# Regrouping the small products of a chunked recurrence and tying its fill work to it, in a hybrid decoder layer

## The chip, the cores and the metric

The kernel runs on one core of one Trainium2 chip. The metric is the time of one execution on the device in microseconds (us), as a median over runs. The inputs are one sequence of 4096 tokens of width 1024, in f32, and the parameters of one layer.

## The reference

One decoder layer with two groups of heads side by side. A normalised input goes through one combined projection. Group A is a recurrence over the tokens (8 heads of 64), group B a dilated sliding-window attention (8 heads of 64). Each is multiplied by a gate from the same projection; both go through an output projection, the residual and a last norm. Cut to what matters:

```python
h = _rmsnorm(x, norm_gain)
p = h @ w_in                       # r, k, v, decay, rate | z_a, q, k, v, z_b
...
def step(S, inp):                  # group A, per head, one token
    sa = einsum('bhvk,bhk->bhv', S, -kk_t)
    S = S * w_t + sa[..., None] * b_t + v_t[..., None] * k_t
    y = einsum('bhvk,bhk->bhv', S, r_t)
    return S, y
...
y_a = group_norm(y) + bonus        # then * silu(z_a)
y_b = dilated_attention(q, k, v)   # (window, dilation) = (128,1), (512,4), (2048,16); then * silu(z_b)
x = rmsnorm(x + concat([y_a, y_b]) @ w_out)
```

## The kernel before, in words

The program is traced into a dependency scheduler, which orders each engine's instructions by their place in the source and by priorities. It has four stages.

The front (to about 650 us) projects the inputs of group A and stores them in DRAM.

The recurrence, `rwkv`, takes the 4096 tokens in 16 iterations of 256, each of 4 chunks c of 64 tokens and 4 pairs p of heads. All its pieces are put into a list of events by `at(t, ...)`, with a nominal time t in units of fill steps; the list is sorted by t and emitted in that order. Pieces of the chain (the inverse, the recurrence's steps, the group norm) are emitted with a raised priority (`HP`), so that the scheduler may place them earlier than the code around them. An iteration has, per pair, the preparation at the offsets of the table `PRE` (`keys`, `decay`, `keys2`, `norms`, `queries`, `gram`, `keysT`, `valuesT`), then `inverse`, which solves a triangular system for each chunk (small products `pq`, L1047 and L1053), then 16 steps s = (c, p) of the chain, then `finish`, the group norm with its transposes `py` (L1120).

`gram(i, st, p, h)` makes the scores of keys and queries within a chunk for one head h of the pair, four products of 64 x 128 rows and columns `pg` (L947), and masks them on VectorE into `G` (L948). The first head uses the upper 64 rows of the array, the second the lower.

A step of the chain, `stage`, has three parts that nominally come one step apart. Part 0 multiplies the state S with the keys and queries KR (L1072, 128 x 128), adds for each head the product GV of masked scores and values (L1074, 64 x 64) and copies the result to Z on ScalarE (L1077). Part 1 copies values to UV (L1081), multiplies Z by the inverse Xn for each head (L1083, 64 x 64) and copies the result to UV (L1085). Part 2 has BKT, keys by UV, as one product of 128 x 128 (L1088), Gout, scores by UV, for each head (L1090, 128 x 64), VectorE's update of S in two halves (L1093), and ScalarE's copy of the outputs into Y (L1095). The three results of a step share one accumulator bank, tag "zy", of which there are 3 (`PSB[2]`).

TensorE's other work in this stage is the fill, `self.fill()`, a generator with 576 steps: projections of the attention's queries, keys and gates in blocks of 24 products `pj` (L737) and of its values in blocks of 24 products `pv` (L718). They accumulate in two banks, tag "proj", and are evacuated by ScalarE and VectorE (for the values `vt`, L728 and L729, and a store `vsc`, L730). The event list takes `UT` = 34 fill steps per iteration; the 32 that are left ("late") follow the last iteration.

Then comes the attention. Its first event closes the fill's memory pools, loads constants (`at`, L1192) and the first head's keys and queries (`km`, `qm`, `kst`, `qhh`), and starts the last gates (weights `wzs`, L347, inputs `xZ`, L353, products `pz`, L357) and the first head's row maxima (`sm`, L1277). The main scores (`st`, L1330 and L1338) follow. The output stage ends the program.

Of the kernel before, what the change touches and what calls it, by code (L numbers as in the profile page):

```python
# [12 lines left out]
F32 = mybir.dt.float32  # L13
# [3 lines left out]
ALU = mybir.AluOpType  # L17
# [35 lines left out]
UVE = 1  # L53
# [6 lines left out]
PRE = (1, 1.5, 3.5, 4, 4.2, 7, 7.2, 9, 9.2)  # L60
# [5 lines left out]
VCE = 0  # L66
# [8 lines left out]
UT = 34  # L75
PSP = 5
# [112 lines left out]
class Layer:  # L189
# [597 lines left out]
    def rwkv(self, then=None):  # L787
# [149 lines left out]
        def gram(i, st, p, h):  # L937

            BK, KR = st["BK", p], st["KR", p]
            if h == 0:  # L940
                st["G", p] = sp.tile([128, 2, NCK, 128], F32, tag="G", name=f"G{i}_{p}", bufs=NG)
            Gt = st["G", p]
            mask = cst[:, C_MASK:C_MASK + 256].rearrange("p (r n) -> p r n", r=2)
            pg = pp.tile([128, NCK, 128], F32, tag="m", bufs=PSB[1], name=f"pg{i}_{p}_{h}")
            hs = slice(h * 64, h * 64 + 64)
            for c in range(NCK):
                P.matmul(pg[:, c, :], lhsT=BK[hs, c, :], rhs=KR[hs, c, :], start=True, stop=True)  # L947
            V.tensor_mul(Gt[:, h].rearrange("p (g r) n -> p g r n", r=2),  # L948
                         pg.rearrange("p (g r) n -> p g r n", r=2),
                         mask[:, None].to_broadcast([128, NCK // 2, 2, 128]))  # L950
            if h == 0:
                return
# [106 lines left out]
        def stage(i, st, s, part):  # L1059

            c, p = s // 4, s % 4
            par = c % 2
            hb, kc = (64, 64) if par == 0 else (0, 0)
            hk, rc = 64 - hb, 64 - kc
            bs, ks = slice(hb, hb + 64), slice(hk, hk + 64)
            KR, Gt, BKT, Vt, WC = (st[x, p] for x in ("KR", "G", "BKT", "V", "WC"))
            halves = [slice(0, 64), slice(64, 128)]
            if part == 0:
                if s == 0:
                    st["Y"] = ip.tile([128, NCK // 2, 512], F32, tag="Y", name=f"Y{i}", bufs=2)  # L1070
                st["bank", s] = bank = pp.tile([128, 3, 128], F32, tag="zy", name=f"zy{i}_{c}_{p}", bufs=PSB[2])
                P.matmul(bank[:, 0], lhsT=KR[:, c, :], rhs=Sbd[p], start=True, stop=True)  # L1072
                for h, hc in enumerate(halves):
                    P.matmul(bank[bs, 0, hc], lhsT=Gt[ks, h, c, kc:kc + 64], rhs=Vt[ks, c // 2, hc],  # L1074
                             start=False, stop=True, skip_group_check=True, tile_position=(hk, hb))
                st["Z", s] = Z = sp.tile([128, 128], F32, tag="Z", name=f"Z{i}_{c}_{p}", bufs=3)
                S.copy(Z[bs], bank[bs, 0])  # L1077
            elif part == 1:
                bank, Z = st["bank", s], st["Z", s]
                st["UV", s] = UV = sp.tile([128, 128], F32, tag="UV", name=f"UV{i}_{c}_{p}", bufs=UVB)  # L1080
                (S.copy, V.tensor_copy, G.tensor_copy)[VCE](UV[ks], Vt[ks, c // 2])  # L1081
                for h, hc in enumerate(halves):
                    P.matmul(bank[bs, 1, hc], lhsT=st["Xn"][bs, p * 4 + h * 2 + c // 2, :], rhs=Z[bs, hc],  # L1083
                             start=False, stop=True, skip_group_check=True, tile_position=(hb, hb))
                (S.copy if UVE else V.tensor_copy)(UV[bs], bank[bs, 1])  # L1085
            else:
                bank, UV = st["bank", s], st["UV", s]
                P.matmul(bank[:, 2], lhsT=BKT[:, c, :], rhs=UV, start=False, stop=True, skip_group_check=True)  # L1088
                for h, hc in enumerate(halves):
                    P.matmul(bank[ks, 0, hc], lhsT=Gt[:, h, c, rc:rc + 64], rhs=UV[:, hc],  # L1090
                             start=False, stop=True, skip_group_check=True, tile_position=(0, hk))
                for hc in halves:
                    V.scalar_tensor_tensor(Sbd[p][hc, hc], Sbd[p][hc, hc], WC[hc, c:c + 1], bank[hc, 2, hc],  # L1093
                                           op0=ALU.mult, op1=ALU.add)
                S.copy(st["Y"][ks, c // 2, p * 128:(p + 1) * 128], bank[ks, 0])  # L1095
# [36 lines left out]
        fill = self.fill()  # L1132
        for i in range(n):
            st = {}
            B = U * i
            for j in range(U):
                at(B + j, next, fill, None)
# [3 lines left out]
            for p in range(4):  # L1141
                b = B + PSP * p
                for o, fn, args in zip(PRE, (keys, decay, keys2, norms, queries, gram, gram, keysT, valuesT),
                                       ((),) * 5 + ((0,), (1,)) + ((),) * 2):
                    at(b + o * PSS, fn, i, st, p, *args)
# [4 lines left out]
            for s in range(16):  # L1150
                for part in range(3):
                    at(t0 + dt * (s + part) + 0.01 * (2 - part), stage, i, st, s, part, hp=HP[1])
# [522 lines left out]
```

## Time and profile before

| | before |
|---|---|
| time, median of 3 runs | 3496.95 us (3493.99 to 3497.66) |
| the profiled execution: time / span | 3487.44 / 3485.7 us |
| mean granted clock of TensorE | 0.948 |
| busy: PE / DVE / ACT / POOL | 3169.3 / 2205.0 / 1874.9 / 1314.9 us |
| products of the fill, pj / pv | 5376 of 277 ns / 768 of 385 ns |
| state L1072 / GV L1074 / Xn L1083 | 512 / 1024 / 1024 passes, 111.2 / 114.7 / 103.3 us busy |
| BKT L1088 / Gout L1090 / gram L947 | 512 / 1024 / 1024 passes, 113.4 / 118.2 / 130.6 us busy |

PE is TensorE's matmuls, PEld its weight loads, DVE is VectorE, ACT ScalarE, POOL GpSimd and SPq SyncE's DMA issues. A row of the time line has the start, the duration, the engine, the source line, the operation, output<-inputs, and how many of them follow each other; square brackets give idle time before it and what ended that. A row of a group has its count, busy time, mean ns of one, and the idle time before. Matmuls are pipelined: a pass shows 220 to 280 ns, while the next begins after about half of that or less, so that lengths are read from one start to the next. An f32 product counts as two passes.

### The profile page before, as it was taken

The page shows a single profiled execution, that of the slowest core. Times are in us where ns is not written, and L with a number is a line of the kernel's source. Part 1 is how long each engine was busy: PE and PEld are TensorE (multiplying, and loading weights), DVE is VectorE, ACT ScalarE, POOL GpSimd, SP SyncE. Part 2 cuts the span into 40 slices and gives each one's busy share as a digit, 9 for nine tenths or more (in the row PEclk, how much of TensorE's full clock was granted, in tenths as well). Part 3 has the DMA queues.
Part 4 walks back from the last instruction along what each step waited for, and adds up shares of the span by engine and source line. Part 5 has one row for each costly group of instructions (what it writes and reads, how often), then busy time and mean ns, then how long its engine had stood idle before and what let it go on. Part 6 is the DMA issues. An engine that isn't in the chain of part 4 may idle for free. (4 is left out here: it accounts for less than half of the span.)

```text
span 3485.7 us, 74535 instructions
## 1 busy us (share of the span) xinstructions
PE 3169.3 (91%) x27788; PEld 2461.5 (71%) x27788; DVE 2205.0 (63%) x5525; ACT 1874.9 (54%) x4174; POOL 1314.9 (38%) x1357
## 2 busy tenths in 40 slices
PE   5989988999999999999999999897988888978788
PEld 4878877878878887888766676675877777833333
DVE  7866767566666777766566677544655555246666
ACT  6465555345655555566555455432666666833233
POOL 4423233232343333333322222201555555755555
PEclk8999999999999999999999999897999999989999
DMA  6243667564455554454533333557755555376563
GB/s 192 92 137 138 198 177 223 194 165 132 123 151 146 153 135 126 126 138 131 157 110 93 99 110 96 123 152 167 132 96 107 111 106 106 100 216 189 185 186 115
DMA packets 644874, 490.59 MB, mean 141 GB/s; under 512 B 329456, under 2 KB 570864, under 8 KB 639472
## 3 DMA queue, kind: packets, MB, share of 16 engines
q1 hardware_dynamic: 644512, 485.83, 51.8%
q8 instruction: 219, 3.59, 0.4%
q14 instruction: 143, 1.17, 0.1%
HBM read 307.65 MB, written 177.77 MB: 139 GB/s over the span
## 5 line engine op out<-in xcount | busy, mean ns | idle before, releaser
L737 PE MATMUL pj<-xF,wf 128*128 128x256 f16 x5376 | 688.6, 277 | 13.4 <-ACT qhl L748 11.3
L737 PEld LDWEIGHTS <-wf 128*128 128x128 f16 x5376 | 502.8, 99 | 109.1 <-issue 14.9
L1350 POOL TENSOR_TENSOR hl<-pt,hl 128x1024 f16<-128x1024 f32 x192 | 367.9, 1926 | 288.6 <-ACT hl L1348 238.6
L562 PEld LDWEIGHTS <-wF 128*128 128x128 f16 x4032 | 395.3, 99 | 98.1 <-issue 42.3
L1590 PE MATMUL o<-wo,yc 128*128 128x512 f16 x1344 | 325.1, 405 | 76.6 <-DVE uC L1610 52.0
L1284 DVE CUSTOM_DVE_ANT_0 jk<-sm,at 128x256 bf16<-128x256 f32 (+1 forms) x768 | 259.1, 389 | 177.4 <-PE sm L1277 175.0
L1341 ACT ACTIVATE pt<-st,pb,esc 128x512 f32<-128x512 f32 (+1 forms) x344 | 257.4, 775 | 195.7 <-PE st L1338 159.4
L1590 PEld LDWEIGHTS <-yc 128*128 128x128 f16 x1344 | 138.0, 104 | 257.9 <-issue 103.7
L562 PE MATMUL ps<-xb,wF 128*128 128x256 f16 x2304 | 280.9, 276 | 23.1 <-DVE c L579 9.4
L1360 PE MATMUL po<-hl,vt 128*128 128x128 f16 (+1 forms) x3528 | 291.5, 234 | 9.9 <-POOL hl L1350 5.2
L1360 PEld LDWEIGHTS <-vt 128*128 128x128 f16 x3528 | 251.7, 101 | 26.9 <-issue 11.1
L1093 DVE SCALAR_TENSOR_TENSOR S<-S,WC,zy 64x64 f32<-64x64 f32 x512 | 142.8, 279 | 196.5 <-PE zy L1090 151.4
L562 PE MATMUL ps<-xa,wF 128*128 128x256 f16 x1728 | 217.8, 276 | 16.3 <-DVE u L577 13.7
L1277 PE MATMUL sm<-km,qm 66*128 66x256 f16 (+1 forms) x768 | 133.4, 279 | 83.5 <-DMA vt<-vsc 40.5
L718 PE MATMUL pv<-wf,xF 128*128 128x512 f16 x768 | 188.5, 385 | 0.0
L1338 PE MATMUL st<-q,k 66*128 66x256 f16 (+1 forms) x768 | 185.0, 271 | 0.0
L1338 PE MATMUL st<-qhh,kst 128*128 128x256 f16 (+1 forms) x768 | 184.5, 270 | 0.0
L1348 ACT CAST hl<-pt 128x1024 f16<-128x1024 f32 x192 | 180.9, 951 | 5.6 <-PE po L1360 3.2
L1277 PEld LDWEIGHTS <-qm 66*128 66x128 f16 x768 | 78.7, 123 | 94.9 <-DMA vt<-vsc 36.0
L1081 ACT COPY UV<-V 64x128 f32<-64x128 f32 x256 | 75.3, 295 | 127.9 <-PE zy L1090 125.3
L1330 PE MATMUL st<-at 128*128 128x512 bf16 (+1 forms) x352 | 136.6, 392 | 1.0 <-ACT pt L1341 0.9
L865 POOL TENSOR_TENSOR l_sq<-sq,h_sq 128x256 fp32r<-128x256 f32 x64 | 54.4, 850 | 219.3 <-ACT h_sq L864 212.3
(287 smaller groups left out, 6953.9 us busy)
## 6 DMA issues: line engine op xcount, KB each, us to landing
xF<-xsc SPq DMA_DIRECT2D x96, 512.0 KB
prs<-o SPq DMA_DIRECT2D x96, 256.0 KB
krv<-prs SPq DMA_DIRECT2D x64, 384.0 KB
wr<-in_w_in_dram SPq DMA_DIRECT2D x33, 512.0 KB
xr<-in_x_dram SPq DMA_DIRECT2D x32, 512.0 KB
xZ<-xsc SPq DMA_DIRECT2D x64, 256.0 KB
gC<-gsc SPq DMA_DIRECT2D x16, 1024.0 KB
xo<-in_x_dram SPq DMA_DIRECT2D x32, 512.0 KB
```

Source lines behind the costliest of these rows:

```text
L562: P.matmul(ps[:, 0:HT], lhsT=w[:, u, q % HK, :], rhs=x[:, v, q % HK, :], start=(start and q == 0), stop=(q == 3 * HK - 1), skip_group_chec ...
L718: P.matmul(ps, lhsT=x[v][:, k, s * 128:(s + 1) * 128], rhs=self.fw["v", 2 * u + k // 4][:, k % 4], start=(q == 0), stop=(q == 23))
L737: P.matmul(ps, lhsT=self.fw[b][:, u, k, :], rhs=x[v][:, k, :], start=(q == 0), stop=(q == 23))
L1093: V.scalar_tensor_tensor(Sbd[p][hc, hc], Sbd[p][hc, hc], WC[hc, c:c + 1], bank[hc, 2, hc], op0=ALU.mult, op1=ALU.add)
L1277: P.matmul(ps[:, n % 2, 256 - w:], lhsT=tok(qm[0:66], d, c, n * 128, 128), rhs=chunks(km[0:66], d, c, lo, w), start=True, stop=True)
L1284: V.tensor_tensor_reduce(jk[:, :w], ps[:, r % 2, 256 - w:], mask[:, i, 256 - w:256], 1.0, -3e38, op0=ALU.add, op1=ALU.max, accum_out=mx[:, ...
L1338: P.matmul(ps[:, at_:at_ + w], lhsT=tok(lh, d, c, n * 128, 128), rhs=chunks(rh, d, c, q0 * 128, w), start=False, stop=not st, skip_group_c ...
L1341: S.activation(pt[:, to:to + at_], ps[:, :at_], AF.Exp, scale=esc[:, p:p + 1], bias=pb[:, 0:1])
L1348: S.copy(hl[:, 0, :n], pt[:, :n])
L1350: (G if nsp[0] % HLG[0] < HLG[1] else V).tensor_sub(hl[:, 1, :n], pt[:, :n], hl[:, 0, :n])
L1360: P.matmul(out, lhsT=v[:, b * VW + v0:b * VW + v0 + 128], rhs=rhs, start=start and v0 + part == 0, stop=True, skip_group_check=True)
L1590: P.matmul(ps, lhsT=x[:, v, q % HK, :], rhs=w[:, u, q % HK, :], start=(start and q == 0), stop=(q == 3 * HK - 1), skip_group_check=True)
```

## The change

Three things are changed. `gram` emits the products of both heads in turn, into two accumulators that it holds at once, and has one place less in `PRE`. The chain's `stage` is split into `with_state`, `solve` and `new_state`, which are emitted slot by slot: state(s), then new_state(s - 2), then `solve` with Xn(s - 1) and GV(s), head by head in turn. In `new_state` BKT becomes two products of 128 x 64; the one of the other half comes first and VectorE updates that half of S, then both Gout products, then BKT of the own half with its update. The last copy of a step, into Y, is kept as `st["out", s]`. And a fill step is taken by `step(i, j)`: within `issue_after`, which makes the ScalarE instructions that it emits stand behind a named instruction, here the Y copy of some step of the iteration before (or of the last step of the one before that). Two options that had one value each are dropped.

```diff
-PRE = (1, 1.5, 3.5, 4, 4.2, 7, 7.2, 9, 9.2)
+PRE = (1, 1.5, 3.5, 4, 4.2, 7, 9, 9.2)
+LEAD = 6
...
-        def gram(i, st, p, h):
+        def gram(i, st, p):
...
-            pg = pp.tile([128, NCK, 128], F32, tag="m", bufs=PSB[1], name=f"pg{i}_{p}_{h}")
-            hs = slice(h * 64, h * 64 + 64)
+            pg = [pp.tile([128, NCK, 128], F32, tag="m", bufs=PSB[1], name=f"pg{i}_{p}_{h}") for h in range(2)]
             for c in range(NCK):
-                P.matmul(pg[:, c, :], lhsT=BK[hs, c, :], rhs=KR[hs, c, :], start=True, stop=True)
+                for h, hs in enumerate((slice(0, 64), slice(64, 128))):
+                    P.matmul(pg[h][:, c, :], lhsT=BK[hs, c, :], rhs=KR[hs, c, :], start=True, stop=True)
...
-                P.matmul(bank[:, 2], lhsT=BKT[:, c, :], rhs=UV, start=False, stop=True, skip_group_check=True)
-                for h, hc in enumerate(halves):
-                    P.matmul(bank[ks, 0, hc], lhsT=Gt[:, h, c, rc:rc + 64], rhs=UV[:, hc],
...
-                for hc in halves:
-                    V.scalar_tensor_tensor(Sbd[p][hc, hc], Sbd[p][hc, hc], WC[hc, c:c + 1], bank[hc, 2, hc],
...
-                S.copy(st["Y"][ks, c // 2, p * 128:(p + 1) * 128], bank[ks, 0])
+            for h in (1 - own, own):
+                hc = halves2[h]
+                if h == own:
+                    for u, uc in enumerate(halves2):
+                        P.matmul(bank[ks, 0, uc], lhsT=Gt[:, u, c, rc:rc + 64], rhs=UV[:, uc],
...
+                P.matmul(bank[hc, 2, hc], lhsT=BKT[:, c, hc], rhs=UV[:, hc], start=False, stop=True,
+                         skip_group_check=True, tile_position=(0, hc.start))
+                V.scalar_tensor_tensor(Sbd[p][hc, hc], Sbd[p][hc, hc], WC[hc, c:c + 1], bank[hc, 2, hc],
+                                       op0=ALU.mult, op1=ALU.add)
+            st["out", s] = S.copy(st["Y"][ks, c // 2, p * 128:(p + 1) * 128], bank[ks, 0])
...
+        def step(i, j):
+
+            s = int((j - LEAD - CHN[0]) / CHN[1]) - 2
+            if s >= 0 and i > 0:
+                after = sts[i - 1].get(("out", s))
+            else:
+                after = sts[i - 2].get(("out", 15)) if i > 1 and j > LEAD else None
+            if after is None:
+                next(fill, None)
+            else:
+                with tc.issue_after(after.ins):
+                    next(fill, None)
...
-                at(B + j, next, fill, None)
+                at(B + j, step, i, j)
...
-            for s in range(16):
-                for part in range(3):
-                    at(t0 + dt * (s + part) + 0.01 * (2 - part), stage, i, st, s, part, hp=HP[1])
+            for s in range(18):
+                if s < 16:
+                    at(t0 + dt * s, with_state, i, st, s, hp=HP[1])
+                if s > 1:
+                    at(t0 + dt * s + 0.01, new_state, i, st, s - 2, hp=HP[1])
+                if s < 17:
+                    at(t0 + dt * s + 0.02, solve, i, st, s, hp=HP[1])
...
-                at(U * n + j, next, fill, None)
+                at(U * n + j, step, n, j)
```

What this makes of the engines' orders is shown at three places. A row names the line, the instruction, its output and its inputs (`zy_1_2` is the accumulator of step c = 1, p = 2; G, UV, BKT its operands), its size, and in brackets the engines for which it waits. The first place is TensorE in the middle of the fill, in iteration 7; before, BKT and Gout of three steps stand between fill products and the gram:

```order
L737 MATMUL pj_16_21245<-xF_0_20689,wf_5_15842 128x256
L1088 MATMUL zy_1_2_20085<-UV_1_2_20110,BKT_2_18373 128x128 [waits Activation_49]
L1090 MATMUL zy_1_2_20085<-UV_1_2_20110,G_2_18318 64x64 x2
L1088 MATMUL zy_1_3_20115<-UV_1_3_20141,BKT_3_18626 128x128 [waits Activation_49]
L1090 MATMUL zy_1_3_20115<-UV_1_3_20141,G_3_18575 64x64 x2
```

After, at the same step of the same iteration:

```order
L944 MATMUL pg_3_1_20113<-KR_3_20009,BK_3_20008 128x128 x3
L736 LDWEIGHTS wf_2_15571
L736 MATMUL pj_23_20536<-xF_0_20392,wf_2_15571 128x256
L1104 MATMUL zy_1_2_20190<-UV_1_2_20230,G_2_18414 64x64 [waits DVE_49]
L1104 MATMUL zy_1_2_20190<-UV_1_2_20230,G_2_18414 64x64
L1106 MATMUL zy_1_2_20190<-UV_1_2_20230,BKT_2_18469 64x64
L1106 MATMUL zy_2_0_20253<-UV_2_0_20314,BKT_0_17971 64x64 [waits Activation_49]
L736 LDWEIGHTS wf_2_15571
L736 MATMUL pj_23_20536<-xF_0_20392,wf_2_15571 128x256
```

Gout now waits for VectorE, and the halves of BKT stand apart, the first of the next step alone ahead of a fill product. The second place is TensorE at the last product of the fill (`pv`, iteration 15). Before:

```order
L718 MATMUL pv_1_30150<-wf_1_23380,xF_1_29862 128x512
L977 MATMUL po_2_28858<-h_rb_2_28737,ones 128x256 [waits Activation_49]
L1088 MATMUL zy_1_0_29026<-UV_1_0_29085,BKT_0_27221 128x128 [waits Activation_49]
L1090 MATMUL zy_1_0_29026<-UV_1_0_29085,G_0_27164 64x64 x2
L1088 MATMUL zy_1_1_29090<-UV_1_1_29138,BKT_1_27410 128x128 [waits Activation_49]
L1090 MATMUL zy_1_1_29090<-UV_1_1_29138,G_1_27380 64x64 x2
```

After:

```order
L717 MATMUL pv_1_30400<-wf_1_23540,xF_1_30103 128x512
L1104 MATMUL zy_1_0_30147<-UV_1_0_30201,G_0_28590 64x64 [waits DVE_49]
L1104 MATMUL zy_1_0_30147<-UV_1_0_30201,G_0_28590 64x64
L1106 MATMUL zy_1_0_30147<-UV_1_0_30201,BKT_0_28643 64x64
L1104 MATMUL zy_1_1_30179<-UV_1_1_30237,G_1_28820 64x64 [waits DVE_49]
L1104 MATMUL zy_1_1_30179<-UV_1_1_30237,G_1_28820 64x64
L1106 MATMUL zy_1_1_30179<-UV_1_1_30237,BKT_1_28851 64x64
L1070 MATMUL zy_1_2_30228<-S_8280,KR_2_28909 128x128 [waits Activation_49]
```

The steps named there are of iteration 14 before (its preparation of iteration 15, `po_2`, is still to come) and of iteration 15 after. The third place is ScalarE at the copies of that last product (`vt`). Before:

```order
L1095 COPY Y_28801<-zy_0_3_28987 64x128 [waits DVE_49]
L728 ACTIVATE vt_1_30226<-pv_1_30150 128x4x64 [waits DMAHW2_49,PE_49]
L1081 COPY UV_1_3_29185<-V_3_27902 64x128 [waits PE_49,Activation_49]
L1081 COPY UV_2_0_29208<-V_0_27226 64x128 [waits PE_49,Activation_49]
L1095 COPY Y_28801<-zy_1_0_29026 64x128 [waits DVE_49]
```

After:

```order
L1110 COPY Y_30013<-zy_1_2_30228 64x128 [waits DVE_49]
L1110 COPY Y_30013<-zy_1_3_30259 64x128 [waits DVE_49]
L1080 COPY UV_2_3_30416<-V_3_29334 64x128 [waits PE_49,Activation_49]
L727 ACTIVATE vt_1_30479<-pv_1_30400 128x4x64 [waits DMAHW5_49]
L1110 COPY Y_30013<-zy_2_0_30295 64x128 [waits DVE_49]
L1092 COPY Z_2_1_30336<-zy_2_1_30320 64x128 [waits PE_49]
L1092 COPY Z_2_2_30366<-zy_2_2_30344 64x128 [waits PE_49]
L727 ACTIVATE vt_1_30479<-pv_1_30400 128x4x64 [waits DVE_49]
```

The copies of the last fill product moved behind Y and Z copies of the chain's last iteration.

More of the change, by code (lines that the diff above doesn't have):

```diff
@@ L52 @@
 MXL = 32
-UVE = 1
 PSB = (2, 2, 3, 1)
@@ L65 @@
 UVB = 3
-VCE = 0
 PRN = 1024
@@ L1057, in inverse, with at_chunk @@
             st["Xn"] = Xn
-        def stage(i, st, s, part):
+        def at_chunk(st, s):
             c, p = s // 4, s % 4
[L1062 to L1072, printed above, removed]
-                for h, hc in enumerate(halves):
[L1074 to L1091, printed above, removed]
-                for hc in halves:
-                    V.scalar_tensor_tensor(Sbd[p][hc, hc], Sbd[p][hc, hc], WC[hc, c:c + 1], bank[hc, 2, hc],
-                                           op0=ALU.mult, op1=ALU.add)
-                S.copy(st["Y"][ks, c // 2, p * 128:(p + 1) * 128], bank[ks, 0])
@@ new lines, in at_chunk, with with_state @@
+            hb, kc = (64, 64) if c % 2 == 0 else (0, 0)
+            return (c, p, slice(hb, hb + 64), slice(64 - hb, 128 - hb), kc) + tuple(
+                st[x, p] for x in ("KR", "G", "BKT", "V", "WC"))
+        halves2 = [slice(0, 64), slice(64, 128)]
+        def with_state(i, st, s):
+            c, p, bs, ks, kc, KR, Gt, BKT, Vt, WC = at_chunk(st, s)
+            if s == 0:
+                st["Y"] = ip.tile([128, NCK // 2, 512], F32, tag="Y", name=f"Y{i}", bufs=2)
+            st["bank", s] = bank = pp.tile([128, 3, 128], F32, tag="zy", name=f"zy{i}_{c}_{p}", bufs=PSB[2])
+            P.matmul(bank[:, 0], lhsT=KR[:, c, :], rhs=Sbd[p], start=True, stop=True)
@@ new lines, in solve @@
+        def solve(i, st, s):
+            for h, hc in enumerate(halves2):
+                if s > 0:
+                    c, p, bs, ks, kc, KR, Gt, BKT, Vt, WC = at_chunk(st, s - 1)
+                    if h == 0:
+                        st["UV", s - 1] = UV = sp.tile([128, 128], F32, tag="UV", name=f"UV{i}_{c}_{p}", bufs=UVB)
+                        S.copy(UV[ks], Vt[ks, c // 2])
+                    P.matmul(st["bank", s - 1][bs, 1, hc], lhsT=st["Xn"][bs, p * 4 + h * 2 + c // 2, :],
+                             rhs=st["Z", s - 1][bs, hc], start=False, stop=True, skip_group_check=True,
+                             tile_position=(bs.start, bs.start))
+                    if h == 1:
+                        S.copy(UV[bs], st["bank", s - 1][bs, 1])
+                if s < 16:
+                    c, p, bs, ks, kc, KR, Gt, BKT, Vt, WC = at_chunk(st, s)
+                    P.matmul(st["bank", s][bs, 0, hc], lhsT=Gt[ks, h, c, kc:kc + 64], rhs=Vt[ks, c // 2, hc],
+                             start=False, stop=True, skip_group_check=True, tile_position=(ks.start, bs.start))
+                    if h == 1:
+                        st["Z", s] = Z = sp.tile([128, 128], F32, tag="Z", name=f"Z{i}_{c}_{p}", bufs=3)
+                        S.copy(Z[bs], st["bank", s][bs, 0])
@@ new lines, in new_state @@
+        def new_state(i, st, s):
+            c, p, bs, ks, kc, KR, Gt, BKT, Vt, WC = at_chunk(st, s)
+            rc = 64 - kc
+            bank, UV = st["bank", s], st["UV", s]
+            own = ks.start // 64
+            for h in (1 - own, own):
[3 more added lines that the diff above has]
+                        P.matmul(bank[ks, 0, uc], lhsT=Gt[:, u, c, rc:rc + 64], rhs=UV[:, uc],
+                                 start=False, stop=True, skip_group_check=True, tile_position=(0, ks.start))
+                P.matmul(bank[hc, 2, hc], lhsT=BKT[:, c, hc], rhs=UV[:, hc], start=False, stop=True,
[3 more added lines that the diff above has]
+            st["out", s] = S.copy(st["Y"][ks, c // 2, p * 128:(p + 1) * 128], bank[ks, 0])
@@ L1142, in rwkv @@
                 b = B + PSP * p
-                for o, fn, args in zip(PRE, (keys, decay, keys2, norms, queries, gram, gram, keysT, valuesT),
-                                       ((),) * 5 + ((0,), (1,)) + ((),) * 2):
-                    at(b + o * PSS, fn, i, st, p, *args)
+                for o, fn in zip(PRE, (keys, decay, keys2, norms, queries, gram, keysT, valuesT)):
+                    at(b + o * PSS, fn, i, st, p)
             gen = inverse(i, st)
```

16 lines of the change are left out of this document (8 added, 8 removed).

## The prediction

> **What bounds the kernel now.** I read the span first, then the engines' busy time by stage, then the time line at both ends of the recurrence's last stretch. The page begins:
>
> ```profile
> span 3485.7 us, 74535 instructions
> ```
>
> The busy time by stage: start and end of the stretch, its us, then for each engine busy us and instructions (PE, PEld, DVE, ACT, POOL), the clock granted to TensorE, DMA share, GB/s.
>
> ```profile
> 650.00:1040.00 390.00, 375.84 (x3511) 313.89 (x3509) 246.70 (x522) 210.22 (x598) 128.22 (x145) 0.98 0.53 143
> 1040.00:1430.00 390.00, 383.29 (x3657) 316.50 (x3656) 276.17 (x582) 226.48 (x662) 131.29 (x143) 0.99 0.51 141
> 1430.00:1820.00 390.00, 381.85 (x3448) 299.61 (x3447) 264.38 (x582) 219.35 (x641) 125.29 (x156) 0.97 0.48 131
> 1820.00:2150.00 330.00, 327.63 (x2634) 226.94 (x2634) 217.96 (x498) 172.08 (x514) 84.51 (x145) 0.99 0.37 104
> 2150.00:2210.00 60.00, 60.00 (x529) 42.48 (x527) 38.75 (x68) 30.36 (x87) 15.86 (x27) 1.00 0.28 75
> 2210.00:2250.00 40.00, 32.66 (x229) 24.98 (x227) 22.44 (x78) 19.18 (x67) 5.27 (x10) 0.76 0.74 127
> 2250.00:2300.00 50.00, 40.68 (x408) 34.15 (x409) 30.14 (x74) 11.61 (x27) 2.90 (x1) 0.85 0.64 184
> 2300.00:2360.00 60.00, 60.00 (x549) 49.12 (x547) 20.52 (x85) 26.26 (x85) 2.90 (x4) 1.00 0.49 138
> 2360.00:2400.00 40.00, 34.68 (x291) 28.75 (x290) 24.51 (x119) 12.80 (x30) 6.38 (x11) 0.89 0.64 186
> ```
>
> From 650 to 2210 us, where the projections (the fill) and the recurrence share TensorE, it is busy 1528.6 of 1560 us: 31 idle. From 2210 to 2400 it is busy 168.0 of 190: 22 idle. The stage that the change touches is bound by TensorE's queue, and 53 us of it are idle. Its two ends, on TensorE:
>
> ```profile
> 2209.43 0.47 PE L977 MATMUL po<-h_rb,ones 128*128 128x256 f32 x1
> ...
> 2399.32 0.61 PE L1330 MATMUL st<-at 128*128 128x512 bf16 x1
> ```
>
> The first row follows the last fill pass, which so ends near 2209.4; the second is the first main score of the attention. I call the 190 us between them the tail. Behind the first main score both kernels have the same work, which I take as unchanged. The time is then the fill's end, the tail and a constant: the change gains only where it takes away work of TensorE, or idle time.
>
> **Part 1, TensorE's work.** Two products on different row halves of the array run at once in the trace: at 1849.16 those of two steps start together, and their eight passes are over by 1849.54, 0.38 us. The 16 gram passes of one head pair, one head behind the other, take 678.22 - 676.57 = 1.65 us, 0.10 each.
>
> ```profile
> 676.57 1.71 PE L947 MATMUL pg<-KR,BK 64*128 64x128 f32 x16
> 678.22 0.83 PE L737 MATMUL pj<-xF,wf 128*128 128x256 f16 x6
> ```
>
> ```profile
> 1849.16 0.27 PE L1083 MATMUL zy<-Z,Xn 64*64 64x64 f32 x1
> 1849.16 0.27 PE L1074 MATMUL zy<-V,G 64*64 64x64 f32 x1
> ...
> 1849.54 0.71 PE L947 MATMUL pg<-KR,BK 64*128 64x128 f32 x4
> ```
>
> The gram is now written with its heads in turn, but the scheduler leaves few pairs so: neighbouring gram products change halves 265 times instead of 47, and 17 of 64 pairs alternate throughout. 218 more changes at one pass of 0.10 are -22 us.
>
> Against that stand the stretches of small products between fill passes. Here are steps of the recurrence in the fill: the first BKT pair comes behind a fill pass, the second behind the column-tiled Gout.
>
> ```profile
> 1501.08 0.39 PE L1088 MATMUL zy<-UV,BKT 128*128 128x128 f32 x2
> 1501.40 0.45 PE L1090 MATMUL zy<-UV,G 128*64 128x64 f32 x4
> 1501.77 0.49 PE L1088 MATMUL zy<-UV,BKT 128*128 128x128 f32 x2
> 1502.19 0.45 PE L1090 MATMUL zy<-UV,G 128*64 128x64 f32 x4
> ```
>
> The first pair takes 1501.40 - 1501.08 = 0.32, the second 1502.19 - 1501.77 = 0.42: leaving a tiled shape costs 0.10. I estimate as much, and a little for a longer first pass, for entering it, 0.23 a stretch. The order has 1009 tiled stretches in the fill before and 1088 after: 79 x 0.23 = +18. [...]
>
> The 256 BKT products of two passes become 512 halves, four passes of half the columns a step. Four Gout passes take 0.37 (1501.77 - 1501.40), two BKT passes 0.32 to 0.42: -0.05 to +0.05 a step, I take +0.02, +5 in all. Sum of the work: -22 + 18 + 5, about 0; with the ends of the last term -15 to +10. The two options that are dropped had the values that the new code writes out: nothing.
>
> **Part 2, work that moves ahead of the last fill pass.** Before, the fill runs ahead of the recurrence: behind its last pass stand 26 steps' worth of products, the inverse of iteration 15 and its last preparation; after, 11 steps' worth and none of the rest. One whole step on TensorE, and the inverse's groups in the tail:
>
> ```profile
> 2222.97 0.44 PE L1083 MATMUL zy<-Z,Xn 64*64 64x64 f32 x4
> 2223.34 0.49 PE L1072 MATMUL zy<-S,KR 128*128 128x128 f32 x2
> ...
> 2224.93 0.66 PE L964 MATMUL pb<-cst,BK 128*128 128x128 f32 x4
> ```
>
> ```profile
> L1047 PE MATMUL pq<-Tn,G 32*32 32x32 f32 x64 | 3.1, 214 | 0.0
> L1053 PE MATMUL pq<-Xn,Tn 32*32 32x32 f32 x64 | 2.9, 193 | 0.0
> ```
>
> The five kinds of product of a step fill 2224.93 - 2222.97 = 1.96 us. 15 x 1.96 = 29.4, the inverse 3.1 + 2.9 = 6.0, and one pair's gram of 1.65 with the transposes and small products of its preparation, which I put at 6 in all: +42 on the fill's end, with 36 to 46. This isn't lost; it leaves the tail.
>
> **Part 3, waits in the fill.** A fill step's ScalarE instructions (its evacuations) now stand behind the Y copy of a step of the iteration before; its loads on SyncE are not tied. ScalarE's queue is in order, so Z and UV copies of the recurrence stand behind a waiting evacuation too, and the next fill block waits for one of two accumulators. In new_state, Gout now waits for VectorE's update of the first half of S, which reads the accumulator that it writes. That update:
>
> ```profile
> L1093 DVE SCALAR_TENSOR_TENSOR S<-S,WC,zy 64x64 f32<-64x64 f32 x512 | 142.8, 279 | 196.5 <-PE zy L1090 151.4
> ```
>
> 0.28 us of work, and I estimate as much again for the way there and back: for 0.6 us TensorE needs other work. Counting TensorE's own work between the instruction that a wait hangs on and the waiting one, 6 waits have under 1.5 us before, and 135 after, 88 of them under 1 us. Where nothing covers such a chain, at the end of the fill, it costs this:
>
> ```profile
> 2241.59 0.80 PE L1072 MATMUL zy<-S,KR 128*128 128x128 f32 x2 [0.50 <-ACT Y L1095]
> ...
> 2245.37 0.80 PE L1072 MATMUL zy<-S,KR 128*128 128x128 f32 x2 [1.03 <-ACT Y L1095]
> ```
>
> Fill passes cover part of it elsewhere; if each of the 88 lacks 0.2 of its 0.6 us, that is 18, and I take +20. The low end is +5, since all such waits hold only 31 us now; the high end 88 x 0.5 = 44, with late evacuations 50.
>
> **Part 4, the new tail.** On SyncE the last values store, the attention's first load and the gates' weights, and on TensorE the first gate product and the group of them:
>
> ```profile
> 2213.70 0.32 SPq L730 DMA_DIRECT2D vsc<-vt  x1
> ...
> 2215.78 0.34 SPq L1192 DMA_DIRECT2D at<-in_attc_dram  x1
> ...
> 2241.46 0.39 SPq L347 DMA_DIRECT2D wzs<-wz  x1
> ```
>
> ```profile
> 2254.95 3.51 PE L357 MATMUL pz<-xZ,wzs 128*128 128x256 f16 x16 [8.17 <-DMA xZ<-xsc]
> ```
>
> ```profile
> L357 PE MATMUL pz<-xZ,wzs 128*128 128x256 f16 x768 | 95.8, 278 | 13.2 <-DMA xZ<-xsc 11.8 <-ACT zhZ L363 1.4
> ```
>
> The last values store comes 4.3 us behind the fill. After, the copies that it waits for stand behind three Y and two Z copies of the last iteration's chain: 9, at worst 15. Then 2 to the first load; from there to the gates' weights it is 25.7 us now, with 35 transfers, among them those of iteration 15's inverse, which wait for data, and 22 transfers after: 15. From the weights to the first gate product 13.5. In all 39, with 34 to 46. All 768 gate products now follow the last recurrence product; before, 528 stand among its last steps. They are 95.8 busy; their 64 loads of 256 KB, 16.8 MB, take 91 us at the 184 GB/s of the stretch from 2250. With the maxima beside them 102 to 118, I take 108, then 10 for the maxima's last waits. 39 + 108 + 10 = 157 instead of 190: -33.
>
> **Sum.** 0 + 42 + 20 - 33 = +29 us: the work stays, the idle time goes from 53 to about 80. The profiled execution took 3487.44 (its span and 1.7 around it), 9.5 below the median of 3496.95; the difference goes on the median: 3526. A measurement of this kernel can tell about 0.2%, 7 us, from no change.
>
> **Rivals.** A, the tail empties more than the waits take: work -10, waits +5, and a tail of 130 (25 to the gates, 102 for them, 3 behind): 42 - 10 + 5 - 60 = -23, 3474. It decides where the tail falls below 190 - 42 less the waits. For it: the granted clock is only 0.76 from 2210 to 2250, so there is time to win. Against it: the gates alone are bound by their loads, and iteration 15 filled that time. Chance 0.16.
>
> B, the regrouped products run side by side: each of 256 steps saves one stretch of 0.37 (2223.34 - 2222.97), -95: 3526 - 95 = 3431. Against it: the order has GV and Xn of neighbouring steps in turn only some 20 times, since Xn waits for ScalarE's Z copy. Chance 0.03. [...]
>
> C, the chain decides: fill that itself waits for the recurrence no longer hides the 88 tight waits, and each costs 1 us, as at 2245.37: +88 instead of +20, 3594. Against it: blocks of 24 fill passes stand ready at most places. Chance 0.10.
>
> D, no difference (3490 to 3504): the fill stretch loses what the tail gains. Chance 0.13.
>
> **How the numbers follow.** The forecast, slower by 7 to 60, has the rest, 0.58. With C slower is 0.68; same 0.13; faster with A and B 0.19. The forecast's own range, its terms' distances added as squares (down 15, 15, 12; up 10, 30, 15), is 3502 to 3561. The range leaves out B, C and under half of A, 0.20: 3475 to 3560.
>
> **What would show it.** Right: the last fill pass near 2270 and the first main score near 2428; some 20 us more idle time of TensorE in the fill, released by S (VectorE) and by Y or Z (ScalarE); all gate products behind the last recurrence product. Wrong: a fill end before 2240 (parts 2 and 3), a tail above 180 or below 140 (part 4), unchanged idle time in the fill (part 3), or a first main score at 2392 or before (the sign).

## The result, and the profile after

The changed kernel takes 3604.13 us (median of 4 runs, 3601.43 to 3615.99) against 3497.3 before: a ratio of 1.030, with a 95% interval of 1.028 to 1.033. The forecast had the sign, slower, but a quarter of the size: 29 us where 107 came, outside its range. The profiled execution after has a span of 3604.0.

Here is the stage that changed, for each kernel in two stretches: from 650 us to the last fill pass, and from there to the first main score (columns as in the prediction). Before:

```profile
650.00:2209.40 1559.40, 1528.01 (x13767) 1198.93 (x13764) 1043.96 (x2250) 858.29 (x2499) 485.16 (x615) 0.98 0.47 129
2209.40:2399.30 189.90, 167.94 (x1470) 137.12 (x1468) 96.92 (x348) 70.03 (x208) 17.46 (x26) 0.89 0.62 158
```

After:

```profile
650.00:2363.00 1713.00, 1633.15 (x14781) 1248.50 (x14778) 1084.81 (x2359) 887.44 (x2596) 490.08 (x630) 0.94 0.44 119
2363.00:2512.00 149.00, 119.85 (x1064) 101.96 (x1062) 55.03 (x249) 41.44 (x115) 6.99 (x14) 0.89 0.69 186
```

Three things are to be read. The fill ends 153.6 us later and the tail is 40.9 shorter; the first main score is 112.7 later, and what follows it 5.6 longer (1086.3 to 1091.9). In the first stretch TensorE is idle 79.9 us where it was 31.4. And its granted clock, the third column from the right, is 0.94 where it was 0.98. In the clock's records of these two traces it is always 1 or one half in this stage; the half adds up to 54.6 us before and 211.6 after. Fill products that follow each other start 0.21 us apart at half clock and 0.11 at full (medians of the trace after), so I take half of the time that TensorE is busy at half clock as lost. It is busy for 51.5 of those 54.6 us and for 187.3 of those 211.6: 25.7 lost before, 93.6 after.

That gives a ledger for every run of this study, from 650 us to the first main score: the idle time of TensorE, the time at half clock, the loss (idle time, and half of the busy time at half clock), and the rest, which is the work at full clock. For before: 53.4 idle, 96.7 at half clock (18.0 of it idle, which is counted already), loss 92.7, work 1656.6. After: 109.0 idle, 243.0 at half clock (43.5 of it idle), loss 208.8, work 1653.2. The loss grew by 116.1, the work shrank by 3.4, and their sum is the 112.7. A second kernel with the same order of TensorE (the state product behind new_state, below) has 7.0 more loss and 8.3 less work than the changed kernel, so differences below 10 us in the ledger say nothing.

One place of the changed kernel, on VectorE and TensorE, shows waits and the half clock that follows them:

```profile
861.80 1.89 DVE L1023 TENSOR_TENSOR pm<-XL,XH 128x1024 f32<-128x1024 f32 x1
...
862.96 0.33 PE L1106 MATMUL zy<-UV,BKT 128*64 128x64 f32 x2
863.60 0.27 DVE L1108 SCALAR_TENSOR_TENSOR S<-S,WC,zy 64x64 f32<-64x64 f32 x1
...
863.93 0.45 PE L1104 MATMUL zy<-UV,G 128*64 128x64 f32 x4 [0.65 <-DVE S L1108]
...
865.25 0.39 PE L1104 MATMUL zy<-UV,G 128*64 128x64 f32 x3 [0.39 <-DVE S L1108]
...
866.54 0.80 PE L1070 MATMUL zy<-S,KR 128*128 128x128 f32 x2 [0.73 <-ACT Y L1110]
...
881.84 5.42 PE L736 MATMUL pj<-xF,wf 128*128 128x256 f16 x27
```

The first half of BKT is done by 863.29; VectorE's update of S could follow, but stands behind an operation of the inverse that starts at 861.80 and takes 1.89, and Gout waits for the update. Within 4 us TensorE waits 0.65, 0.39 and 0.73. The clock falls at 866.1, during the third wait; the state product of 866.54 takes 0.80 where the median at full clock is 0.49 in this stretch. The clock in the three stretches around it:

```profile
862.70:866.10 3.40, 2.08 (x23) 1.39 (x21) 3.37 (x6) 0.75 (x3) 0.00 (x0) 1.00 0.00 0
866.10:886.60 20.50, 20.06 (x143) 15.74 (x144) 10.96 (x25) 11.61 (x34) 5.25 (x10) 0.50 0.26 56
886.60:906.60 20.00, 20.00 (x237) 17.13 (x236) 9.26 (x21) 12.65 (x36) 9.02 (x6) 1.00 0.59 165
```

After 1.32 us idle of 3.40 the clock is at half for 20.5 us, in which TensorE is busy 20.06: by the half taken above 10 us are lost, behind waits of 1.8. From the fall to 881.84 TensorE has only f32 products of the recurrence and its preparation; there a block of 27 fill products begins, and 4.8 us later the clock is full. All 19 such periods of the first stretch after, and 10 of the 11 before, have at least 0.36 us of idle time in the 8 us ahead of them; of the stretches of 8 us at full clock, taken every 2 us, 90 of 674 after and 60 of 708 before have as much. The waits of TensorE by what they wait for, first one row from before, then after:

```profile
PE zy L1072 <- ACT Y L1095: 1.9, 2, 1.5
```

```profile
PE zy L1070 <- ACT Y L1110: 24.7, 22, 3.4
PE pg L944 <- DVE BK L917: 10.6, 3, 8.7
PE zy L1104 <- DVE S L1108: 9.2, 14, 2.2
```

The state product's wait for the Y copy, which frees its accumulator, was 1.9 us before; Gout's wait for S did not exist.

### The profile page after: what moved, and what is told of

It reads as the page before. It is cut to its first block, busy times and chain, and to the rows that moved or that the text cites. A ratio compares the mean times of both kernels' runs of the same rounds, so it can differ in the third digit from the quotient of the medians.

```text
span 3604.0 us, 75138 instructions
## 1 busy us (share of the span) xinstructions
PE 3217.6 (89%) x28300; PEld 2465.9 (68%) x28300; DVE 2194.6 (61%) x5525; ACT 1873.3 (52%) x4174; POOL 1316.8 (37%) x1357
## 5 line engine op out<-in xcount | busy, mean ns | idle before, releaser
L736 PE MATMUL pj<-xF,wf 128*128 128x256 f16 x5376 | 708.8, 280 | 5.0 <-ACT qhl L747 4.1
L561 PE MATMUL ps<-xb,wF 128*128 128x256 f16 x2304 | 285.2, 278 | 26.0 <-DVE c L578 10.2
L1108 DVE SCALAR_TENSOR_TENSOR S<-S,WC,zy 64x64 f32<-64x64 f32 x512 | 137.1, 279 | 196.6 <-PE zy L1106 187.3
L1311 PE MATMUL sm<-km,qm 66*128 66x256 f16 (+1 forms) x768 | 130.8, 277 | 79.9 <-DMA kst<-qk 18.2
L1070 PE MATMUL zy<-S,KR 128*128 128x128 f32 x512 | 123.1, 324 | 28.0 <-ACT Y L1110 25.7
L1106 PE MATMUL zy<-UV,BKT 128*64 128x64 f32 x1024 | 144.5, 239 | 1.7 <-ACT UV L1085 1.7
L911 POOL TENSOR_TENSOR BK<-kk,sg 128x256 f32<-128x256 f32 x64 | 61.1, 955 | 221.1 <-DVE sg L887 176.2
```

Of the source, the lines that this page charges most:

```text
L561: P.matmul(ps[:, 0:HT], lhsT=w[:, u, q % HK, :], rhs=x[:, v, q % HK, :], start=(start and q == 0), stop=(q == 3 * HK - 1), skip_group_chec ...
L736: P.matmul(ps, lhsT=self.fw[b][:, u, k, :], rhs=x[v][:, k, :], start=(q == 0), stop=(q == 23))
L1106: P.matmul(bank[hc, 2, hc], lhsT=BKT[:, c, hc], rhs=UV[:, hc], start=False, stop=True, skip_group_check=True, tile_position=(0, hc.start))
```

## The experiments

The theory behind the runs: new bare waits of the chain, in its new order (1) or for want of fill where it is tied (2), bring idle time and with it half clock. The first four runs do each part alone, and all but the tie. The ratio is that to the kernel before on the same chip.

**The gram in turn, alone.**

```diff
-        def gram(i, st, p, h):
+        def gram(i, st, p):
...
+                for h, hs in enumerate((slice(0, 64), slice(64, 128))):
+                    P.matmul(pg[h][:, c, :], lhsT=BK[hs, c, :], rhs=KR[hs, c, :], start=True, stop=True)
```

> The kernel before with the gram's two heads in turn and nothing else. Theory 1 (the chain's new order makes the waits) and theory 2 (the tied fill makes them) expect the same here: the gram is no cause of the loss, 3475 to 3500 against 3497 before, with idle time of TensorE in the fill stretch of 25 to 40 us (31 before). A rival, that two accumulators held at once by one gram starve the preparation (tag m has two), expects over 3520 and waits of the gram on VectorE.

Measured 3473.2 against 3498.3, ratio 0.994 (0.992 to 0.996): 25 us faster, a little more than expected of it. The ledger has 22.9 less work. The rival of starved preparation, which expected over 3520, is out by the time; idle time in the fill is 43.5, just above the range expected.

**The chain's new order, alone.**

```diff
-                for part in range(3):
-                    at(t0 + dt * (s + part) + 0.01 * (2 - part), stage, i, st, s, part, hp=HP[1])
+            for s in range(18):
+                if s < 16:
+                    at(t0 + dt * s, with_state, i, st, s, hp=HP[1])
...
```

> The kernel before with the chain's new order (with_state, solve, new_state) alone: fill untied, gram by head. Theory 1 expects most of the loss: 3550 to 3600, over 60 us idle in the fill stretch, waits of the state product on ScalarE's Y copy and of Gout on VectorE's S, and over 150 us at half clock (55 before). Theory 2 expects 3485 to 3515 and idle time near 31, since untied fill still covers the waits.

Measured 3535.4, ratio 1.012 (1.010 to 1.015). Neither theory had it. The first stretch and the tail of this run:

```profile
650.00:2117.30 1467.30, 1445.89 (x13375) 1119.40 (x13372) 949.26 (x2073) 788.36 (x2299) 428.38 (x562) 0.99 0.48 132
2117.30:2457.90 340.60, 297.30 (x2499) 237.47 (x2498) 186.77 (x558) 138.27 (x413) 58.52 (x73) 0.76 0.45 110
```

With the fill untied, the scheduler fills the chain's waits with more fill: the first stretch has only 21.4 us idle and ends 92 us earlier. But 51 steps of the recurrence are left behind the last fill pass, and there the waits are bare: clock 0.76, tail 341 us. The cost of the new order is real, and moves to where the fill is not.

**The tie, alone.**

```diff
-                at(B + j, next, fill, None)
+                at(B + j, step, i, j)
...
-                S.copy(st["Y"][ks, c // 2, p * 128:(p + 1) * 128], bank[ks, 0])
+                st["out", s] = S.copy(st["Y"][ks, c // 2, p * 128:(p + 1) * 128], bank[ks, 0])
```

> The kernel before with the fill tied to the Y copies alone: chain and gram as before. Theory 1 expects 3490 to 3520: the fill's end later by some 40, the tail shorter by as much, idle time in the fill below 45. Theory 2 expects 3560 to 3600, with over 60 us idle and over 150 us at half clock, waits of fill products on ScalarE's evacuations among them.

Measured 3569.8, ratio 1.020 (1.016 to 1.024), as theory 2 expects:

```profile
650.00:2337.00 1687.00, 1612.87 (x14228) 1262.25 (x14226) 1090.83 (x2349) 886.98 (x2588) 505.76 (x626) 0.96 0.45 120
2337.00:2486.80 149.80, 122.77 (x1060) 103.22 (x1058) 57.33 (x255) 44.19 (x123) 8.17 (x16) 0.89 0.67 187
```

With the chain as before, the tie brings 74.1 us idle in the first stretch and the late end. The loss of the ledger grows by 75.9, the work by 11.6, hardly more than the ledger can tell; the first main score comes 87.5 later.

**The gram and the chain, fill untied.** The changed kernel with one line back:

```diff
-                at(B + j, step, i, j)
+                at(B + j, next, fill, None)
```

> The changed kernel with its fill untied (gram and chain as changed). Theory 1 expects 3550 to 3590; theory 2 expects 3480 to 3505; if both are needed (the chain's bare waits hurt only where the fill is held back), 3490 to 3520 here and the same in the two runs with one of them alone.

Measured 3532.0, ratio 1.011 (1.008 to 1.013), between the theories. Against this run the tie costs 73 us more. So the loss has two causes of its own, and theory 1 or 2 alone is not enough.

The next runs take up the chain's order. **The state product behind new_state:**

```diff
-                    at(t0 + dt * s, with_state, i, st, s, hp=HP[1])
+                    at(t0 + dt * s + 0.015, with_state, i, st, s, hp=HP[1])
```

> The changed kernel, with the state product of step s emitted behind new_state(s - 2) and not ahead of it. Theory 1a: the state product waits bare because only one solve stands between the Y copy that frees its accumulator and itself; with BKT and Gout in between, the waits of the state product on ScalarE's Y copy fall from 24.7 us to under 8, idle time in the fill from 80 to 60, half clock from 212 to 140 to 170, and the time from 3604 to 3545 to 3575. Theory 2 (the tied fill alone makes the idle time) expects no change, 3590 to 3615.

Measured 3613.4, ratio 1.031 (1.028 to 1.033): no gain, and the waits for Y are 25.3 us as before. But the run tells nothing of theory 1a: TensorE's order is the changed kernel's, instruction by instruction; the scheduler seems to place these products by priority and readiness and not by their place in the list. It is a second measurement of the changed kernel and shows how far two such agree (3604 and 3613). Theory 1a stays untested.

**BKT whole, Gout and both updates behind it**, the slots as changed:

```diff
+            P.matmul(bank[:, 2], lhsT=BKT[:, c, :], rhs=UV, start=False, stop=True, skip_group_check=True)
             for u, uc in enumerate(halves2):
                 P.matmul(bank[ks, 0, uc], lhsT=Gt[:, u, c, rc:rc + 64], rhs=UV[:, uc],
...
-                P.matmul(bank[hc, 2, hc], lhsT=BKT[:, c, hc], rhs=UV[:, hc], start=False, stop=True,
```

> The changed kernel with BKT again as one product, then Gout, then both updates of S; slots, gram and tie as changed. Theory 1b (Gout's wait for VectorE's update of the first half, which delays the Y copy and with it the next state product): the 9.2 us of Gout's waits go, those of the state product halve, 3550 to 3580. Theory 2 expects 3590 to 3615.

Measured 3544.1, ratio 1.011 (1.008 to 1.013): 60 us faster than the changed kernel. Gout's waits are gone, those for Y fall to 13.4. Idle time as a whole hardly falls (77.3 in the first stretch), since other waits grow, but the time at half clock does, from 211.6 to 122.9. Theory 1b holds, with a time just below its range; what Gout's wait costs comes mostly through the clock, and not through idle time.

Then the tie. **Only its far end** (the last Y copy two iterations back) **and only its near one:**

```diff
-            if s >= 0 and i > 0:
-                after = sts[i - 1].get(("out", s))
-            else:
-                after = sts[i - 2].get(("out", 15)) if i > 1 and j > LEAD else None
+            if True:
+                after = sts[i - 2].get(("out", 15)) if i > 1 and j > LEAD else None
```

> The kernel before with the fill tied only to the last Y copy two iterations back (from the seventh fill step of an iteration on). If the near tie makes the cost: 3495 to 3515, idle time in the fill 30 to 45, half clock 50 to 80. If any tie that stops the fill from running ahead costs: 3545 to 3575, as in the run with both.

```diff
-                after = sts[i - 2].get(("out", 15)) if i > 1 and j > LEAD else None
+                after = None
```

> The kernel before with the fill tied only to the Y copies of the last iteration's steps 0 to 8 (the fill steps from the 23rd on, and the late ones). If the near tie makes the cost: 3545 to 3580, with over 60 us idle and over 120 us at half clock in the fill. If the far one does: 3495 to 3520.

Measured 3595.6, ratio 1.025 (1.023 to 1.028), and 3569.9, ratio 1.019 (1.016 to 1.021). Each by itself costs about as much as both together or more (91 and 65 us, against 72), in the first stretch 68.7 and 70.0 idle and 177.5 and 150.2 at half clock. It isn't how near the tie is.

**The tie on TensorE's Gout and not on ScalarE's Y copy:**

```diff
-                    P.matmul(bank[ks, 0, hc], lhsT=Gt[:, h, c, rc:rc + 64], rhs=UV[:, hc],
+                    st["out", s] = P.matmul(bank[ks, 0, hc], lhsT=Gt[:, h, c, rc:rc + 64], rhs=UV[:, hc],
...
```

> The kernel before with the same tie as in the run with the tie alone, but fill steps stand behind the step's last Gout product on TensorE instead of its Y copy on ScalarE: TensorE's fill products are held back, ScalarE's queue is free. If holding the fill back costs: 3550 to 3585, idle time in the fill over 60 us. If it was ScalarE's queue (evacuations behind copies that wait, and Z and UV behind those): 3495 to 3525, idle time below 45 and waits of fill products on ScalarE near the 13 us of before.

Measured 3579.9, ratio 1.021 (1.018 to 1.024), with 78.0 idle and 139.9 at half clock. ScalarE's queue behind a waiting evacuation, which part 3 named, is not needed for the cost; the fill held back costs by itself.

**BKT whole and the fill untied:** the edits of two runs above together.

> The changed kernel with BKT whole (Gout behind it, then both updates) and the fill untied; the gram in turn and the slots stay. If the halves of BKT make the chain's cost: 3465 to 3485, as the gram alone (3473). If the slots make it (state ahead of new_state, heads in turn): 3520 to 3540, as with the halves and no tie (3532).

Measured 3501.0, ratio 1.000 (0.998 to 1.002), between the two expected. The slots give back the gram's 25 us, and the halves with the wait cost some 33 more, up to the ratio of the run with halves and no tie. Against this run the tie, with BKT whole, costs only 39 us (ratio 1.011 against 1.000).

**Gout first, then both halves of BKT, then both updates**, all else as changed:

```diff
             for u, uc in enumerate(halves2):
                 P.matmul(bank[ks, 0, uc], lhsT=Gt[:, u, c, rc:rc + 64], rhs=UV[:, uc],
                          start=False, stop=True, skip_group_check=True, tile_position=(0, ks.start))
+            for hc in halves2:
+                P.matmul(bank[hc, 2, hc], lhsT=BKT[:, c, hc], rhs=UV[:, hc], start=False, stop=True,
+                         skip_group_check=True, tile_position=(0, hc.start))
```

> The changed kernel with Gout ahead of both halves of BKT and the two updates behind them: the halves stay, the round trip over VectorE between them and Gout goes. If the round trip costs: 3535 to 3555, as with BKT whole (3544). If the halves themselves do (twice the passes, more stretches of small products): 3590 to 3610. An even split would be 3565 to 3580.

Measured 3518.1, ratio 1.004 (1.002 to 1.006), faster than any price named. The halves are not the cost; here, with no wait between them and Gout, they are a gain (3518.1 against 3544.1 with BKT whole). On TensorE, a step in the fill:

```profile
1502.40 0.27 PE L1100 MATMUL zy<-UV,G 128*64 128x64 f32 x1
1502.41 0.27 PE L1103 MATMUL zy<-UV,BKT 128*64 128x64 f32 x1
...
1502.68 0.28 PE L1103 MATMUL zy<-UV,BKT 128*64 128x64 f32 x2
1502.89 0.50 PE L736 MATMUL pj<-xF,wf 128*128 128x256 f16 x3
```

Passes of Gout and of the BKT half in the other columns start 10 to 20 ns apart where they stand in turn and run side by side: the eight take 0.49 us (1502.40 to 1502.89). Before, two whole BKT passes and four of Gout take 0.69 (0.32 + 0.37 in the prediction's rows) to 0.79. The ledger has 80.8 less work than before. It also has more idle time, 133.1, presumably because less work covers the same waits.

So two more runs take this into the kernel before, untied, in part 2 of its own stage. **With the gram, and without it:**

```diff
-                P.matmul(bank[:, 2], lhsT=BKT[:, c, :], rhs=UV, start=False, stop=True, skip_group_check=True)
                 for h, hc in enumerate(halves):
...
+                for hc in halves:
+                    P.matmul(bank[hc, 2, hc], lhsT=BKT[:, c, hc], rhs=UV[:, hc], start=False, stop=True,
+                             skip_group_check=True, tile_position=(0, hc.start))
```

> The kernel before with the gram's heads in turn and, in part 2 of its own stage, Gout ahead of two halves of BKT, both updates behind them; fill untied. If four Gout passes and four half passes of BKT run side by side in 0.49 us, as in the run with Gout first, and not in 0.79: 256 x 0.28 = 72 less than the gram alone, 3400 to 3435. If untied fill then runs so far ahead that the recurrence ends bare at half clock (39 steps behind the last fill pass), only half of it: 3435 to 3470.

> The kernel before with Gout ahead of the halves of BKT alone: 3420 to 3450 if the side-by-side passes give 72 us also without the gram in turn; 3480 to 3510 if they give what the longer bare end takes away.

Measured 3487.5, ratio 0.996 (0.994 to 0.997), and 3477.3, ratio 0.993 (0.991 to 0.996). The first is above both ranges expected, the second just below the later one (0.79 - 0.49 is 0.30 and not 0.28: 77 us for 256 steps). Both are faster than before, as is the gram alone, but by 16 and 26 us where the work falls by 80.5 and 65.1. The rest is lost again: the tail grows to 259 and 249 us with 39 steps in it, at a granted clock of 0.82 and 0.81, and the loss of the ledger from 92.7 to 155.4 and 135.5. On top of the gram alone (0.994) the halves gain nothing.

Last, theory 3: waits last up to 2 us since VectorE's update stands behind the inverse's long operations. **These in halves**, in the changed kernel, with the tie alone, and with the halves of BKT alone:

```diff
-PRN = 1024
+PRN = 512
```

> The changed kernel with the inverse's products on VectorE cut into halves (each some 1.0 us where it was 1.9 to 2.0, and twice as many). Theory 3: Gout's wait is long because VectorE's update of S stands behind such an operation. Then the waits of Gout on S fall from 9 to about 5 us and those of the state product on Y from 25 to about 15, and the time from 3604 to 3560 to 3590. If the long operations are no cause: 3600 to 3620, since more operations cost VectorE more.

> The kernel before with the tie alone and the same shorter operations. Theory 3 expects 3540 to 3560 against 3570 with the tie alone; if the tie's idle time has other causes, 3565 to 3580.

> The kernel before with Gout ahead of the halves of BKT (3477) and the shorter operations. Theory 3 expects 3455 to 3472, the idle time behind the fill smaller; otherwise 3475 to 3490.

Measured 3614.9, ratio 1.031 (1.028 to 1.035); 3589.8, ratio 1.024 (1.022 to 1.027); 3487.5, ratio 0.996 (0.993 to 0.998). None is faster than its partner. In the changed kernel the waits for Y do fall, from 24.7 to 14.6 us, and Gout's stay at 9.7, but the inverse's own products wait longer (12.9 for 7.2) and idle time as a whole rises to 86.6. Theory 3 explains the rows shown, not the time.

By each run's distance to its own before, the 107 us are: the gram -25, the slots +26 (to the run with BKT whole and untied), the halves with VectorE's update between them +33, the tie on top +73. The split hangs on the order: with the tie ahead of the halves, the tie is +39 and the halves +67, so each costs about twice as much where the other is there. The ledger, from 650 us to the first main score ("of it idle" is idle time at half clock; the last column is read below):

| run | fill end | first score | idle | at half clock | of it idle | loss | work | windows without fill |
|---|---|---|---|---|---|---|---|---|
| before | 2209.4 | 2399.3 | 53.4 | 96.7 | 18.0 | 92.7 | 1656.6 | 14 |
| after | 2363.0 | 2512.0 | 109.0 | 243.0 | 43.5 | 208.8 | 1653.2 | 60 |
| gram alone | 2183.1 | 2380.1 | 52.8 | 90.0 | 2.9 | 96.4 | 1633.7 | 13 |
| chain alone | 2117.3 | 2457.9 | 64.7 | 202.2 | 41.0 | 145.3 | 1662.6 | 15 |
| tie alone | 2337.0 | 2486.8 | 101.2 | 178.6 | 43.7 | 168.6 | 1668.2 | 45 |
| gram, chain, untied | 2123.4 | 2454.5 | 75.3 | 184.7 | 42.4 | 146.5 | 1658.0 | 11 |
| after, state product behind | 2364.1 | 2510.7 | 110.2 | 261.6 | 50.5 | 215.8 | 1644.9 | 61 |
| after, BKT whole | 2297.3 | 2446.7 | 105.1 | 154.2 | 42.6 | 160.8 | 1635.9 | 34 |
| far tie alone | 2335.0 | 2490.2 | 76.5 | 230.0 | 11.3 | 185.8 | 1654.4 | 52 |
| near tie alone | 2332.5 | 2486.3 | 100.6 | 185.5 | 41.5 | 172.6 | 1663.7 | 54 |
| tie on Gout | 2337.7 | 2480.4 | 105.7 | 168.0 | 43.4 | 168.0 | 1662.4 | 44 |
| after, BKT whole, untied | 2210.1 | 2401.8 | 60.1 | 92.2 | 4.3 | 104.1 | 1647.7 | 16 |
| after, Gout first | 2281.5 | 2429.4 | 133.1 | 193.1 | 52.0 | 203.6 | 1575.8 | 48 |
| gram, halves, Gout first | 2122.3 | 2381.5 | 93.2 | 156.4 | 32.0 | 155.4 | 1576.1 | 12 |
| halves alone, Gout first | 2127.8 | 2377.0 | 68.7 | 160.1 | 26.6 | 135.5 | 1591.5 | 10 |

**What the half clock follows.** In the fill of all 18 traces (the 15 of this table and the three with the inverse in halves), the clock changes only on a grid of 3.413 us; every change lies within 0.002 us of it. So each such window can be counted by its idle time and by the fill products that start in it. The table says how many of the windows are followed by one at half clock:

| the window | no fill product | 1 to 9 | 10 and more |
|---|---|---|---|
| at full clock, under 0.3 us idle | 9 of 194 | 8 of 1789 | 0 of 5100 |
| at full clock, 0.3 to 1.5 us idle | 58 of 87 | 35 of 119 | 1 of 318 |
| at full clock, over 1.5 us idle | 63 of 64 | 71 of 77 | 12 of 40 |
| at half clock, under 0.3 us idle | 145 of 157 | 64 of 130 | 2 of 172 |

So in these counts idle time alone does not tell of half clock: 0.3 to 1.5 us of it are followed by half clock in 58 of 87 windows without a fill product, and in 1 of 318 with ten or more. Nor does the want of fill alone (9 of 194). Of the windows already at half clock, with TensorE idle for under 0.3 us, 145 of 157 without a fill product are followed by another at half, and 2 of 172 with ten or more; the period of 866.1 ended 4.8 us behind the first fill product, at 881.84. The tie makes windows without them: before has 14 of 455, the other untied runs 10 to 16, the tied ones 34 to 74, the changed kernel 60 of 500. Those 60 hold 46.0 of its 79.9 us idle in the fill; before, the 14 hold 4.1 of 31.4. This is counted in the traces and not set by a run; what sets the f32 products of the recurrence apart from the fill here, their shape, their type or their number, is open.

## Why the prediction was wrong, point by point

**Part 1, about 0.** The work fell by 3.4, which is less than the ledger can tell. The gram term was right (-22, against -25 in time and -23 in work). The 18 for the stretches was not measured by itself. That the halves of BKT cost 5 was wrong as a property of theirs: next to Gout they save some 65 (alone) to 77 (in the changed kernel). The row for it was not in the trace before, and the rows at 1849.16, which show row halves side by side, were read for the gram and not for columns.

**Part 2, +42.** Right. The tail lost 40.9 us with 7.2 more idle time and 7.5 less of loss to half clock, so 40.6 of work left it.

**Part 4, a tail of 157.** 149. The gates begin 42.1 us behind the fill (2405.1), where 39 were reckoned.

**Part 3, +20: the step that failed.** It priced a wait at the time that TensorE stands still, took a fifth of a microsecond for each of 88, and let fill cover the rest. Idle time in the fill rose by 48.5 us, to the range's upper end. Beyond that there was no term for the clock, which lost 67.9 us more there: 116 in all where 20 stood. A row with such a price stands in the prediction: from 2210 to 2250, with 7.3 of 40 us idle, the granted clock is 0.76; TensorE is busy for 13.9 of the 19.0 us at half clock, a loss of 7.0 us more. It was read as time to be won in rival A and not as the price of a wait. With the measured idle time and this ratio of 0.95, part 3 would have come to 95. The cover failed too: that blocks of fill stand ready at most places, which spoke against rival C, doesn't hold where 60 of 500 windows have no fill product.

The 22 waits of the state product for Y last at most 3.4 us each. The rows at 863.93 to 866.54 have gaps of 0.65, 0.39 and 0.73 us, and 20.5 us at half clock follow them. What followed such gaps in these traces differs with the fill products beside them, by the counts above.

**The rivals.** C had the size, 3594, and the reason that held-back fill no longer hides the waits, but not the way: there are 22 waits for Y of 1.1 us and 14 of Gout of 0.7, and not 88, and the rest of the cost is the clock. A's short tail of 130 did not come (149, nearer to the 157 of the forecast), nor did its waits of +5. B was right that regrouped products can run side by side, in a place it did not look at (eight passes in 0.49 us with Gout first), and the changed order keeps them apart.

**What stays open.** That a tie of any kind, near or far, on ScalarE or on TensorE, costs 65 to 91 us on the chain of before is shown, as is where the time goes; with gram, slots and BKT whole it costs 39. Why held-back fill leaves more idle time is shown in part: of the rise in the fill, 42 of 48.5 us in the changed kernel and 35 of 42.7 with the tie alone lie in windows without a fill product, but only 10 of 37.3 with the far tie alone. The waits themselves are spread over many pairs of engines (the largest, with the tie alone, is 13.6 us of gram products waiting for their keys). And no run sets idle time or fill by itself, so what brings the half clock is read from the counts of windows and from the ledger.

## What to carry to other kernels

Price a wait of TensorE by its own length and by the clock behind it: here a microsecond of idle time in the fill cost another 0.5 to 1.2 at half clock, by the run, so the rows to look for are those where the granted clock is under 1 between full stretches. Work that fills waits should not be held back to where the chain ends (the tie alone came to a ratio of 1.020 here); run-ahead that looks wasteful is the cover, and where it is spent the chain's end is bare (a tail of 341 us at a clock of 0.76 with the chain alone). Small products on different column halves paid here only when no other engine's step lay between them (3518.1 against 3604.1), so put the products of a step together first, and the updates that read the same accumulator behind.

## What the runs showed of the hardware that was not expected

Products of 128 x 64 on the two column halves ran side by side even into the same accumulator: with Gout first, eight passes in 0.49 us at 1502.40, starts 10 to 20 ns apart. The 19 periods at half clock in the fill after last multiples of 3.4 us (3.4, 6.8, 10.2, 13.7, 17.1, 20.5, 23.9 and 37.5). The one of 866.1 follows gaps of 0.39 to 0.73 us and lasts 20.5, with TensorE busy for 20.06 of them; it ended 4.8 us behind the first fill product of a block.
